# A hand-set opening of a fused decoder block: v's parts and two blocks of q moved ahead of mem's values, norm factors and keys

## The chip, the cores and the metric

The kernel runs on one core of one Trainium2 chip. The metric is the device time of one execution in microseconds (us), as the median of several executions. The profile is of one such execution. PE is the matmul engine, PEld its weight loads, ACT the scalar engine, DVE the vector engine, POOL GpSimd, SP the engine that issues most transfers.

## The reference

One decoder layer over 256 positions of 1024 features, with 256 memory tokens:

```
h    = rmsnorm(x, g_pre_mix)
proj = h @ w_in            # cb, cc, cv, q, k, v (512 columns each), qm (512), three gates (1024 each)
y_a  = (cb * causal_dwconv(cc * cv)) @ w_conv_out
y_b  = attention(q, k, v: 8 heads of 64, causal, position bias) @ w_attn_out
mem_n = rmsnorm(mem, g_mem);  mk, mv = split(mem_n @ w_mem_kv)
y_c  = attention(qm, mk, mv: 4 heads of 128, no mask) @ w_mem_out
x    = x + rmsnorm((sig(ga)*y_a + sig(gb)*y_b + sig(gc)*y_c) @ w_out, g_post_mix)
u    = causal_dwconv(rmsnorm(x, g_pre_ffn) @ w_up);  a, g = split(u)
out  = x + rmsnorm((gelu(a) * g) @ w_down, g_post_ffn)
```

The sequence is one block long, so the block selection of the attention has nothing to select: each query sees its own block.

## The kernel before

**Arithmetic.** Every operand of a matmul is held as two parts, hi (rounded) and lo (the rest). `hilo` makes them: ACT writes hi, then DVE writes lo = value - hi. A product is hi·hi + hi·lo + lo·hi. `wide_blocks` makes a block of 128 output features: 8 matmuls of 512 columns with the weights' hi part (line 237), 8 of 256 columns with their lo part (line 239). After it `add_up` brings the two halves together: ACT copies one half out (`t`, line 244) and DVE adds the other (line 245). After every second block the caller's `evac` runs; `q_evac` is 2 ACT copies (line 502) and 2 DVE operations (line 503).

**Weights.** They come as a list of pieces, in the order of use: 0 to 7 are the memory values' weights, 8 to 11 the memory keys', 12 to 15 v's, 16 to 19 q's (one block each), 20 to 23 k's, 24 to 27 those of the memory queries. `split_until` makes a piece's two parts (line 211 on ACT, line 212 on DVE); five buffers hold the parts of normal pieces, so piece n takes the buffer of piece n - 5. `weights()` is called once for each piece used and asks for the splits of the next three pieces as well; in v's loop it asks for two. Raw pieces are loaded by SP, two in a transfer, and from piece 18 on into three buffers in turn.

**The first stretch.** A region set by hand (`manual_schedule`, from line 421) fixes the order of PE, ACT and DVE *among the instructions written inside it*. Where instructions written behind it fall between them is left to the scheduler of the framework, which draws up each engine's order when the kernel is built; at run time each engine issues in that order. Inside the region stand: the memory values (`pmv`, 2 accumulators), x's norm and its transposes into `hT`, the memory keys (`mk_raw`), and v (`pv`, line 468). Then come, on lines 469 to 478:

- `rm`: two squares of `m_sb` on ACT (line 288) with two small POOL operations each: 1/rms of each memory token
- `mv`: `pmv` scaled by `rm`, as hi and lo (lines 260, 264)
- `spread(diagonals(rm))`: DVE makes two diagonal tiles `dg` (line 296), PE multiplies each with ones (`sp`, line 303; each shows as two matmul records), DVE copies the result to `rms` (line 305)
- `mk`: the two pairs of raw keys times `rms` (line 476), as hi and lo; then `bgh` (line 478)

**Behind the region**, and so placed by the scheduler: two POOL memsets and the load of `bias`, v's parts `vp` in the tile `vk` (`hilo` of `pv`, lines 260 and 262), the four blocks of q and the four of k (lines 513, 514), then the attention's heads with the remaining projections as filler between their steps. The first PE work of the heads is `sc` (lines 537, 538), in the accumulators that `pmv` and `pv` used.

Of the kernel before, what the change touches and what calls it, by code (L numbers as in the profile page):

```python
# [11 lines left out]
F32 = mybir.dt.float32  # L12
F32R = mybir.dt.float32r
BF16 = mybir.dt.bfloat16
AF = mybir.ActivationFunctionType
ALU = mybir.AluOpType
# [3 lines left out]
P = 128  # L20
D = 1024
S = 256
KT = D // P
NT = S // P
H = 8
DH = 64
HM = 4
CW = 512
# [68 lines left out]
def trunk(ctx, tc, x, mem, memT_in, weights_in, par_in, bias_in, g_post_mix, g_post_ffn, out):  # L97
    nc = tc.nc
    const = ctx.enter_context(tc.tile_pool(name="const", bufs=1))
    sb = ctx.enter_context(tc.tile_pool(name="sb", bufs=1))  # L100
# [5 lines left out]
    def tok(t):  # L106
        return slice(t * P, (t + 1) * P)

    def f32(ap):
        return ap.bitcast(F32)  # L110

    def bank(name="mm"):
        return ps.tile([P, 512], F32, tag="mm", name=name, bufs=4)
# [4 lines left out]
    def parts_tile(n, tag, name):  # L118

        return sb.tile([P, n, 2, S], F32R, tag=tag, name=name).rearrange("p k a s -> p a k s")  # L120
# [94 lines left out]
    def weights(hold=False, ahead=AHEAD):  # L215

        nonlocal used, freed
        if not hold:
            freed = used
        split_until(used + 1 + ahead)  # L220
        used += 1
        return parts[used - 1]
# [9 lines left out]
    def mm_wide(p, wh, wl, a):  # L232


        kt = wh.shape[1]
        for k in range(kt):
            nc.tensor.matmul(p, wh[:, k], a[:, :, k], start=(k == 0), stop=False)  # L237
        for k in range(kt):
            nc.tensor.matmul(p[:, :S], wl[:, k], a[:, 0, k], start=False, stop=(k == kt - 1))  # L239

    def add_up(dst, p, tag="t", bufs=2):

        t = wk.tile([P, S], F32, tag=tag, name="t", bufs=bufs)
        nc.scalar.activation(t, p[:, S:], AF.Copy)  # L244
        nc.vector.tensor_tensor(dst, p[:, :S], t, ALU.add)  # L245
# [12 lines left out]
    def hilo(hi, lo, src, scale=1.0):  # L258

        nc.scalar.activation(hi, src, AF.Copy, scale=scale)  # L260
        if isinstance(scale, float) and scale == 1.0:
            nc.vector.tensor_tensor(lo, src, f32(hi), ALU.subtract)
        else:
            nc.vector.scalar_tensor_tensor(lo, src, scale, f32(hi), op0=ALU.mult, op1=ALU.subtract)

    def small(name, n=1):
        return wk.tile([P, n], F32, tag=f"small{n}", name=name, bufs=8)
# [17 lines left out]
    def rstd_row(src, name):  # L285
        ss, se, r = small("ss"), small("se"), small(name)
        junk = wk.tile([P, D], F32, tag="pT", name="junkd", bufs=2)
        nc.scalar.activation(junk, src, AF.Square, scale=D ** -0.5, accum_out=ss)
        nc.gpsimd.tensor_scalar(se, ss, EPS, None, op0=ALU.add)
        nc.gpsimd.tensor_tensor(r, se, mhalf, op=ALU.pow)  # L290
        return r
# [60 lines left out]
    def wide_blocks(nb, a, evac, dst=None):  # L352

        y, wh, wl = None, None, None
        for b in range(nb):
            if wh is None:
                wh, wl = weights()
                at = 0
            p = bank("ft")
            mm_wide(p, wh[:, :, at:at + P], wl[:, :, at:at + P], a)  # L360
            at += P
            if at == wh.shape[2]:
                wh = None
            if b % 2 == 0:
                y = wk.tile([P, 2, S], F32, tag="y", name="y", bufs=YB) if dst is None else dst[:, b:b + 2]
            add_up(y[:, b % 2], p)
            if b % 2:
                evac(b - 1, y)
            yield
# [14 lines left out]
    def run(gen):  # L384
        for _ in gen:
            pass
# [9 lines left out]
    hT = parts_tile(KT, "B", "hT")  # L396
# [12 lines left out]
    with tc.manual_schedule(engines={mybir.EngineType.SP}):  # L409
        for what in "w0 w1 w2 w3 m46 w4 w5 m68 w6 w7 w8 x0 x1 w9 p w10 w11 w12 w13 t0 t1".split():  # L410
            if what[0] == "m":
                a, b = (KT + int(c) * S for c in what[1:])
# [5 lines left out]
            else:  # L418
                t = int(what[1])
                nc.sync.dma_start((x_sb if what[0] == "x" else m_sb)[:, t], (x if what[0] == "x" else mem)[tok(t)])  # L420
    with tc.manual_schedule(engines={mybir.EngineType.PE, mybir.EngineType.Activation, mybir.EngineType.DVE}):
        nc.scalar.activation(small("preload"), mhalf, AF.Exp)
        pw = bank("pw")

        def keep_warm(n):
            one = nc.const_aps.tensor(1.0, (P, 512), BF16)
            for _ in range(n):
                nc.tensor.matmul(pw, one[:, :P], one, start=True, stop=True)

        def mem_part(k):  # L430
            hilo(memT[:, 0, k], memT[:, 1, k], rawT[:, k], gm[:, k:k + 1])

        keep_warm(9)
        nc.vector.tensor_scalar_mul(memT[:, 0, 0], rawT[:, 0], gm[:, 0:1])
        nc.vector.scalar_tensor_tensor(memT[:, 1, 0], rawT[:, 0], gm[:, 0:1], f32(memT[:, 0, 0]), op0=ALU.mult,
                                       op1=ALU.subtract)
        split_until(1)
        mem_part(1)
        split_until(2)
        for k in range(KT):  # L440
            wh, wl = weights(ahead=1)
            if k == 0:
                for n, (a, w) in enumerate(((0, wh), (1, wh), (0, wl))):
                    for t in range(NT):
                        nc.tensor.matmul(pmv[t], memT[:, a, 0, tok(t)], w[:, 0], start=(n == 0), stop=False)
            else:
                values(pmv, memT, k, wh[:, 0], wl[:, 0])
            if k + 2 < KT:
                mem_part(k + 2)
                split_until(k + 3)  # L450
        rx = [rstd_row(x_sb[:, 0], "rx")]
        split_until(9)
        rx.append(rstd_row(x_sb[:, 1], "rx"))
        for t in range(NT):
            nc.vector.tensor_scalar_mul(xn[:, t], x_sb[:, t], rx[t])
            split_until(10 + t)
        gen = blocks(4, memT, mk_evac)
        next(gen)
        next(gen)
        scaled(hT, turned(xn, range(0, 4)), gp)  # L460
        next(gen)
        scaled(hT, turned(xn, range(4, KT)), gp)
        run(gen)
        pv = acc("pv")
        for k in range(0, KT, 2):
            wh, wl = weights(ahead=2)
            for j in range(2):
                values(pv, hT, k + j, wh[:, j], wl[:, j])
        rm = [rstd_row(m_sb[:, t], "rm") for t in range(NT)]
        mv = sb.tile([P, 2, NT, CW], F32R, tag="E", name="mv")  # L470
        for t in range(NT):
            hilo(mv[:, 0, t], mv[:, 1, t], pmv[t], rm[t])
        rms = spread(diagonals(rm), "rms")
        mk = sb.tile([P, 2, HM, S], F32R, tag="mk", name="mk")
        for b, y in zip(range(0, HM, 2), mk_raw):
            nc.vector.tensor_tensor(y, y, twice(rms), ALU.mult)
            hilo(mk[:, 0, b:b + 2], mk[:, 1, b:b + 2], y)
        nc.vector.tensor_scalar_mul(bgh, bg, 0.5)


    vk = sb.tile([P, 4, 1024], F32R, tag="A", name="vk")
    vp = vk[:, :2].rearrange("p a (t c) -> p a t c", c=CW)
    kl = vk[:, 2:].rearrange("p j (n s) -> p j n s", s=S)
    bias = sb.tile([P, H, S], F32, tag="bias", name="bias")
    with tc.manual_schedule(engines={mybir.EngineType.Pool}):
        for j, r in enumerate((slice(0, DH), slice(DH, P))):
            nc.gpsimd.memset(f32(kl[r, 1 - j]), 0.0)
        nc.gpsimd.dma_start(bias, bias_in)
    for t in range(NT):
        hilo(vp[:, 0, t], vp[:, 1, t], pv[t])  # L490

    qk = sb.tile([P, 2, 4, 2, S], F32R, tag="C", name="qk")
    q2, k2 = qk[:, 0], qk[:, 1]
    HEAD = (slice(0, DH), slice(DH, P))

    def q_evac(b, p):
        for j, r in enumerate(HEAD):  # L500
            hi, src = q2[r, b:b + 2, j], p[r]
            nc.scalar.activation(hi, src, AF.Copy, scale=DH ** -0.5)
            nc.vector.scalar_tensor_tensor(q2[HEAD[1 - j], b:b + 2, j], src, DH ** -0.5, f32(hi), op0=ALU.mult,
                                           op1=ALU.subtract)

    def k_evac(b, p):
        for j, r in enumerate(HEAD):
            hi, src = k2[r, b:b + 2, j], p[r]
            nc.scalar.activation(hi, src, AF.Copy)
            nc.vector.tensor_tensor(kl[r, j, b:b + 2], src, f32(hi), ALU.subtract)  # L510
            nc.vector.tensor_copy(k2[HEAD[1 - j], b:b + 2, j], f32(hi))

    run(wide_blocks(4, hT, q_evac))
    run(wide_blocks(4, hT, k_evac))


# [15 lines left out]
    def attend(pair):  # L532
# [30 lines left out]
        mm3(two(po)[:, :, P:], v[1], [pT1[:, b].rearrange("p (j s) -> p j s", s=P) for b in range(2)], False, True)  # L563
        for j, r in enumerate(HEAD):
            hilo(oT[r, 0, pair], oT[r, 1, pair], two(po)[r, j])
# [289 lines left out]
```

## Time and profile before

| | us |
|---|---|
| median of 3 executions (lowest, highest) | 447.78 (447.72, 448.78) |
| the profiled execution | 447.71 |
| its span, first to last instruction | 445.8 |
| PE busy in it | 434.2 |
| PE idle by the page (445.8 - 434.2) | 11.6 |

The span is 1.9 us shorter than the execution's own time. "Busy" of PE is modelled from pipelined matmuls, so the start times of neighbouring matmuls are the better clock.

### The profile page before, as it was taken

What the parts mean: (1) busy time and instruction counts of PE and PEld (TensorE: products, weight loads), DVE (VectorE), ACT (ScalarE), POOL (GpSimd) and SP (SyncE); (2) the same over time, 40 slices, a digit from 0 to 9 for tenths busy, and PEclk for the clock granted to TensorE, in tenths of its full rate; (3) what the DMA queues carried; (4) which work ended last, traced back from release to release, by engine and by line L of the source; (5) the groups of instructions that cost most, each with busy time, mean ns of one, the idle gap of its engine ahead of it and who ended that gap; (6) DMA issues with size and microseconds to landing.
All of it is one profiled execution on the core that took longest, in us unless ns stands there. A gap on an engine that the chain in (4) does not pass through costs nothing.

```text
span 445.8 us, 6664 instructions
## 1 busy us (share of the span) xinstructions
PE 434.2 (97%) x2423; PEld 375.4 (84%) x2423; DVE 358.2 (80%) x634; ACT 292.5 (66%) x526; POOL 13.2 (3%) x35
## 2 busy tenths in 40 slices
PE   8998999999999999999999899999999999999994
PEld 4997888888888988888888698888888888888883
DVE  5787889869986787798686679997879878878875
ACT  6787676757677766666655568866657657657642
POOL 0121000000000000000000300000000000000001
PEclk9999999999999999999999999999999999999998
DMA  8997454543535453455857046556556546546102
GB/s 273 410 419 295 150 191 161 190 160 128 185 122 196 156 187 109 177 190 190 278 193 285 1 159 224 185 188 201 187 182 200 190 176 202 190 175 206 79 1 94
DMA packets 14288, 83.38 MB, mean 187 GB/s; under 512 B 1584, under 2 KB 2096, under 8 KB 5424
## 3 DMA queue, kind: packets, MB, share of 16 engines
q1 hardware_dynamic: 13536, 80.34, 50.5%
q10 hardware_dynamic: 576, 1.58, 1.1%
q0 software_dynamic: 144, 1.05, 0.6%
q8 instruction: 19, 0.31, 0.3%
q14 instruction: 13, 0.11, 0.1%
HBM read 81.91 MB, written 1.05 MB: 186 GB/s over the span
## 4 chain that ended last, share of the span: by engine, by line
PE 95%; ACT 1%; DVE 1%; DMA 1%; issue 0%; POOL 0%; POOLq 0%; DVEq 0%; ACTq 0%
PE ft L237 42%; PE ft L239 21%; PE pf L251 13%; PE po L251 5%; PE pmv L251 2%; PE pv L251 2%; PE po L256 1%; DMA raw<-in_weights_dram 1%; PE ft L229 1%; PE ft L228 1%; PE ft L230 1%; PE at L256 1%; ACT wh L211 1%; PE tp L315 1%; PE ft L377 0%
## 5 line engine op out<-in xcount | busy, mean ns | idle before, releaser
L211 ACT ACTIVATE wh<-raw 128x1024 fp32r<-128x1024 f32 (+1 forms) x139 | 143.3, 1034 | 103.7 <-PE ft L237 71.5
L212 DVE TENSOR_TENSOR wl<-raw,wh 128x1024 fp32r<-128x1024 f32 (+1 forms) x139 | 165.4, 1192 | 53.5 <-ACT wh L211 51.7
L237 PE MATMUL ft<-hT,wh 128*128 128x512 f32 x384 | 97.3, 393 | 0.0
L237 PE MATMUL ft<-h2T,wh 128*128 128x512 f32 x328 | 82.2, 392 | 0.0
L237 PEld LDWEIGHTS ft<-hT,wh 128*128 128x128 f32 x384 | 68.9, 189 | 12.2
L237 PEld LDWEIGHTS ft<-h2T,wh 128*128 128x128 f32 x328 | 59.5, 189 | 11.0
L239 PEld LDWEIGHTS ft<-hT,wl 128*128 128x128 f32 x384 | 52.2, 190 | 3.7
L239 PE MATMUL ft<-hT,wl 128*128 128x256 f32 x384 | 53.6, 282 | 0.0
L244 ACT ACTIVATE t<-ft 128x256 f32<-128x256 f32 x116 | 42.9, 372 | 10.4 <-PE ft L239 10.3
L251 PE MATMUL pf<-wh,f 128*128 128x512 f32 x176 | 49.2, 390 | 0.0
L239 PEld LDWEIGHTS ft<-h2T,wl 128*128 128x128 f32 x328 | 44.9, 190 | 3.3
L239 PE MATMUL ft<-h2T,wl 128*128 128x256 f32 x328 | 45.9, 282 | 0.0
L251 PEld LDWEIGHTS pf<-wh,f 128*128 128x128 f32 x176 | 32.4, 188 | 6.2
L245 DVE TENSOR_TENSOR y<-ft,t 128x256 f32<-128x256 f32 x68 | 28.2, 419 | 2.9 <-ACT t L244 2.6
L251 PE MATMUL pf<-wl,f 128*128 128x512 f32 x88 | 27.5, 390 | 0.0
L748 ACT ACTIVATE u<-v,par 128x256 f32<-128x256 f32 x44 | 24.0, 589 | 3.8 <-DVE v L742 3.8
L597 DVE SCALAR_TENSOR_TENSOR u<-v,par,u 128x255 f32<-128x255 f32 x44 | 19.7, 479 | 0.7 <-ACT u L748 0.7
L598 DVE SCALAR_TENSOR_TENSOR u<-v,par,u 128x254 f32<-128x254 f32 x44 | 19.7, 478 | 0.1
L251 PEld LDWEIGHTS pf<-wl,f 128*128 128x128 f32 x88 | 16.5, 188 | 3.5
L245 DVE TENSOR_TENSOR v<-ft,t 128x256 f32<-128x256 f32 x44 | 18.0, 418 | 0.5 <-ACT t L244 0.5
L251 PE MATMUL po<-wh,mg 128*128 128x512 f32 x64 | 17.9, 389 | 0.0
L251 PEld LDWEIGHTS po<-wh,mg 128*128 128x128 f32 x64 | 11.9, 188 | 2.4
(175 smaller groups left out, 534.8 us busy)
## 6 DMA issues: line engine op xcount, KB each, us to landing
raw<-in_weights_dram SPq DMA_DIRECT2D x66, 1024.0 KB, 4.8
raw<-in_weights_dram SPq DMA_DIRECT2D x8, 256.0 KB, 5.4
rawx<-in_weights_dram SPq DMA_DIRECT2D x4, 512.0 KB, 9.0
rawx<-in_weights_dram SPq DMA_DIRECT2D x2, 1024.0 KB, 12.5
raw<-in_weights_dram SPq DMA_DIRECT2D x2, 512.0 KB, 7.3
x_sb<-in_x_dram SPq DMA_DIRECT2D x2, 512.0 KB, 7.4
m_sb<-in_mem_dram SPq DMA_DIRECT2D x2, 512.0 KB, 9.8
bias<-in_bias_dram POOLq DMA_DIRECT2D x1, 1024.0 KB, 8.9
```

The source lines that it names most:

```text
L211: nc.scalar.activation(hi, v, AF.Copy)
L212: nc.vector.tensor_tensor(lo, v, f32(hi), ALU.subtract)
L228: nc.tensor.matmul(dst, wh[:, k], ah[:, k], start=(k == 0), stop=False)
L237: nc.tensor.matmul(p, wh[:, k], a[:, :, k], start=(k == 0), stop=False)
L239: nc.tensor.matmul(p[:, :S], wl[:, k], a[:, 0, k], start=False, stop=(k == kt - 1))
L244: nc.scalar.activation(t, p[:, S:], AF.Copy)
L245: nc.vector.tensor_tensor(dst, p[:, :S], t, ALU.add)
L251: nc.tensor.matmul(d, a, w[:, c:c + 512], start=(first and w is wh and a is ah), stop=(last and a is al))
L256: nc.tensor.matmul(dst, a[i], b[j], start=(first and n == 0), stop=(last and n == 2))
L597: nc.vector.scalar_tensor_tensor(t[:, 1:], src[:, :S - 1], w1, t[:, 1:], op0=ALU.mult, op1=ALU.add)
L598: nc.vector.scalar_tensor_tensor(t[:, 2:], src[:, :S - 2], w0, t[:, 2:], op0=ALU.mult, op1=ALU.add)
L748: nc.scalar.activation(d, v[:, i], AF.Identity, bias=bb, scale=w2)
```

## The change

The definitions of `vk`, `bias`, `qk`, `q_evac` and `k_evac` move up into the hand-set region. In it, v's parts and the first two blocks of q (with their splits of weights, `add_up` and one `q_evac`) now stand between the squares of `m_sb` and `mv`. The last two blocks of q and all of k stay behind the region. No operation is added or taken away.

```diff
@@ -467,6 +467,40 @@
                 values(pv, hT, k + j, wh[:, j], wl[:, j])
         rm = [rstd_row(m_sb[:, t], "rm") for t in range(NT)]
+        vk = sb.tile([P, 4, 1024], F32R, tag="A", name="vk")
+        vp = vk[:, :2].rearrange("p a (t c) -> p a t c", c=CW)
+        kl = vk[:, 2:].rearrange("p j (n s) -> p j n s", s=S)
+        bias = sb.tile([P, H, S], F32, tag="bias", name="bias")
+        with tc.manual_schedule(engines={mybir.EngineType.Pool}):
+            for j, r in enumerate((slice(0, DH), slice(DH, P))):
+                nc.gpsimd.memset(f32(kl[r, 1 - j]), 0.0)
+            nc.gpsimd.dma_start(bias, bias_in)
...
+        qk = sb.tile([P, 2, 4, 2, S], F32R, tag="C", name="qk")
...
+        for t in range(NT):
+            hilo(vp[:, 0, t], vp[:, 1, t], pv[t])
+        gen = wide_blocks(4, hT, q_evac)
+        next(gen)
+        next(gen)
         mv = sb.tile([P, 2, NT, CW], F32R, tag="E", name="mv")
         for t in range(NT):
             hilo(mv[:, 0, t], mv[:, 1, t], pmv[t], rm[t])
@@ -476,41 +510,7 @@
         nc.vector.tensor_scalar_mul(bgh, bg, 0.5)
-
-
-    vk = sb.tile([P, 4, 1024], F32R, tag="A", name="vk")
...
-    for t in range(NT):
-        hilo(vp[:, 0, t], vp[:, 1, t], pv[t])
...
-    run(wide_blocks(4, hT, q_evac))
+    run(gen)
     run(wide_blocks(4, hT, k_evac))
```

## Rows read from the trace of the kernel before

**Rows 1.** the page: busy time, and the chain that ended last

```profile
PE 434.2 (97%) x2423; PEld 375.4 (84%) x2423; DVE 358.2 (80%) x634; ACT 292.5 (66%) x526; POOL 13.2 (3%) x35
...
PE 95%; ACT 1%; DVE 1%; DMA 1%; issue 0%; POOL 0%; POOLq 0%; DVEq 0%; ACTq 0%
```

**Rows 2.** stretches: length, busy us (instructions) by engine, granted clock, DMA share

```profile
41.50:43.50 2.00, 0.70 (x5) 0.47 (x4) 2.00 (x5) 1.82 (x3) 0.00 (x0) 1.00 0.56 139
43.50:84.00 40.50, 40.50 (x239) 35.69 (x238) 36.20 (x73) 27.11 (x50) 0.00 (x0) 1.00 0.49 175
84.00:90.00 6.00, 5.86 (x36) 4.99 (x35) 4.93 (x14) 4.36 (x10) 0.00 (x0) 1.00 0.53 178
```

**Rows 3.** timeline of PE: start, length, what, count, idle before and its releaser

```profile
41.37 0.39 PE L251 MATMUL pv<-wh,hT 128*128 128x512 f32 x1
43.06 0.46 PE L303 MATMUL sp<-dg,ones 128*128 128x128 f32 x2 [1.30 <-DVE dg L296]
43.27 2.09 PE L237 MATMUL ft<-hT,wh 128*128 128x512 f32 x8
45.20 1.11 PE L239 MATMUL ft<-hT,wl 128*128 128x256 f32 x8
...
46.38 0.38 PE L303 MATMUL sp<-dg,ones 128*128 128x128 f32 x2
...
49.18 2.00 PE L237 MATMUL ft<-hT,wh 128*128 128x512 f32 x8
...
54.76 2.00 PE L237 MATMUL ft<-hT,wh 128*128 128x512 f32 x8
```

**Rows 4.** timeline of ACT around the end of v

```profile
39.08 1.06 ACT L211 ACTIVATE wh<-raw 128x1024 fp32r<-128x1024 f32 x1 [0.57 <-PE pv L251]
40.04 1.25 ACT L260 ACTIVATE mv<-pmv,rm 128x512 fp32r<-128x512 f32 x2
41.18 1.21 ACT L260 ACTIVATE vk<-pv 128x512 fp32r<-128x512 f32 x2
...
46.36 0.37 ACT L244 ACTIVATE t<-ft 128x256 f32<-128x256 f32 x1
...
53.03 1.27 ACT L502 ACTIVATE qk<-y 64x512 fp32r<-64x512 f32 x2
```

**Rows 5.** timeline of DVE before and behind the end of v

```profile
32.47 3.55 DVE L212 TENSOR_TENSOR wl<-rawx,wh 128x1024 fp32r<-128x1024 f32 x3 [0.57 <-ACT wh L211]
37.50 1.22 DVE L212 TENSOR_TENSOR wl<-raw,wh 128x1024 fp32r<-128x1024 f32 x1 [1.48 <-ACT wh L211]
40.17 1.23 DVE L212 TENSOR_TENSOR wl<-raw,wh 128x1024 fp32r<-128x1024 f32 x1 [1.45 <-ACT wh L211]
41.31 1.40 DVE L264 SCALAR_TENSOR_TENSOR mv<-pmv,rm,mv 128x512 fp32r<-128x512 f32 x2
42.63 0.47 DVE L296 TENSOR_SCALAR dg<-ident,rm 128x128 f32<-128x128 f32 x2
43.02 1.28 DVE L262 TENSOR_TENSOR vk<-pv,vk 128x512 fp32r<-128x512 f32 x2
44.22 1.21 DVE L212 TENSOR_TENSOR wl<-raw,wh 128x1024 fp32r<-128x1024 f32 x1
```

**Rows 6.** groups of DVE from 42 to 72: count, busy, mean ns, idle before

```profile
L212 DVE TENSOR_TENSOR wl<-raw,wh 128x1024 fp32r<-128x1024 f32 x10 | 12.2, 1224 | 3.2 <-ACT wh L211 3.1
L245 DVE TENSOR_TENSOR y<-ft,t 128x256 f32<-128x256 f32 x9 | 3.8, 419 | 0.0
...
L296 DVE TENSOR_SCALAR dg<-ident,rm 128x128 f32<-128x128 f32 x2 | 0.5, 278 | 0.0
```

**Rows 7.** waits of PE over the whole span: us in total, times, longest

```profile
PE sp L303 <- DVE dg L296: 1.3, 1, 1.3
...
PE ft L237 <- DVE y L245: 0.2, 1, 0.2
```

**Rows 8.** page, part 6: a load of two pieces, us to landing

```profile
raw<-in_weights_dram SPq DMA_DIRECT2D x66, 1024.0 KB, 4.8
```

More of the change, by code (lines that the diff above doesn't have):

```diff
@@ L469, in trunk, with q_evac, k_evac @@
         rm = [rstd_row(m_sb[:, t], "rm") for t in range(NT)]
+        vk = sb.tile([P, 4, 1024], F32R, tag="A", name="vk")
[7 more added lines that the diff above has]
+        qk = sb.tile([P, 2, 4, 2, S], F32R, tag="C", name="qk")
+        q2, k2 = qk[:, 0], qk[:, 1]
+        HEAD = (slice(0, DH), slice(DH, P))
+        def q_evac(b, p):
+            for j, r in enumerate(HEAD):
+                hi, src = q2[r, b:b + 2, j], p[r]
+                nc.scalar.activation(hi, src, AF.Copy, scale=DH ** -0.5)
+                nc.vector.scalar_tensor_tensor(q2[HEAD[1 - j], b:b + 2, j], src, DH ** -0.5, f32(hi), op0=ALU.mult,
+                                               op1=ALU.subtract)
+        def k_evac(b, p):
+            for j, r in enumerate(HEAD):
+                hi, src = k2[r, b:b + 2, j], p[r]
+                nc.scalar.activation(hi, src, AF.Copy)
+                nc.vector.tensor_tensor(kl[r, j, b:b + 2], src, f32(hi), ALU.subtract)
+                nc.vector.tensor_copy(k2[HEAD[1 - j], b:b + 2, j], f32(hi))
+        for t in range(NT):
[3 more added lines that the diff above has]
+        next(gen)
         mv = sb.tile([P, 2, NT, CW], F32R, tag="E", name="mv")
@@ L478, in trunk @@
         nc.vector.tensor_scalar_mul(bgh, bg, 0.5)
-    vk = sb.tile([P, 4, 1024], F32R, tag="A", name="vk")
[L482 to L488, printed above, removed]
-    for t in range(NT):
-        hilo(vp[:, 0, t], vp[:, 1, t], pv[t])
[L495 to L511, printed above, removed]
-    run(wide_blocks(4, hT, q_evac))
+    run(gen)
     run(wide_blocks(4, hT, k_evac))
```

## The prediction

> **What bounds the kernel now.** I read the page first: PE is busy for 434.2 us of a span of 445.8, and 95% of the chain that ended last lies on PE [rows 1]. So only time in which PE stands still, or matmuls that go away, can move the end; other engines matter where they make PE wait. Next the list of PE's waits: behind the opening there is one of note before the two sub-layers meet, `sp` waiting 1.3 us for DVE's `dg`; among the blocks the only other is a `ft` matmul with 0.2 us [rows 7]. (Nothing before v moves, and the stop between the two sub-layers and the tail are the same code.) Then the table by stretch, to see whether the engine makes up for that wait: from 41.5 to 43.5 PE is busy for 0.70 of 2.00 us, at full granted clock, and from 43.5 to 84 for 40.50 of 40.50 [rows 2]. A saturated engine has nothing to make it up with, so time won at 41.5 should reach the end, as long as nothing opens behind it.
>
> The timelines tell why it waits. v's last matmul starts at 41.37; matmuls of this size follow each other at 0.23 us, so the next could start at 41.60. It starts at 43.06: 1.46 us lost, of which the view lists 1.30 as idle, since the last matmul's end lies at 41.76 [rows 3]. The matmul that waits is `sp`, in its hand-set place. Behind it on PE stands q's first block, and that could have run: its weight parts are among three splits that DVE ended at 36.02 [rows 5], and all of v's matmuls have read `hT` already. What `sp` waits for is a string of steps: ACT splits a piece at 39.08, when v's matmuls give up its buffer; then ACT writes `mv` from 40.04 to 41.29 [rows 4], DVE writes mv's lo parts from 41.31 and `dg` from 42.63, the first of the two ending near 42.9 [rows 5].
>
> **The change, part by part.** Operations stay the same in number and size, so the sum has only order in it.
>
> *Two q blocks ahead of `sp` on PE.* They need nothing that is late, so q's first block starts at 41.60 in place of 43.27 less the two `sp` records. Gain: 1.46 us. Its lower bound by the view's own idle is 1.30; I take 1.46, from start to start.
>
> *`sp` behind them.* The two products of 0.46 and 0.38 us [rows 3] stay and cost what they did. The question is their wait. A block takes 2.79 us (49.18 to 54.76 for two) [rows 3], so q's second block is issued by 41.60 + 5.58 = 47.18. `mv` now stands behind that block's `q_evac` on ACT and DVE. Before, q's first block began at 43.27 and ACT took its result at 46.36, 3.09 later [rows 3, 4]; so here ACT takes the second at 41.60 + 2.79 + 3.09 = 47.48. From there: `t` 0.37, DVE's sum 0.42, `q_evac` on ACT 1.27 for two, `mv` on ACT 1.25 for two, the last lo part of `mv` 0.7, the first `dg` 0.28 [rows 4, 5, 6], together 4.29, and some 0.15 for the hand-overs: `dg` is there at about 51.9. If PE's order has `sp` directly at 47.18, PE stands for 4.7 us; behind q's third block (49.97) for 1.9; behind the fourth (52.76) not at all. The third and fourth blocks are the scheduler's to place, and it does place such work between hand-set instructions: the second `sp` stands at 46.38 behind 17 matmuls of q, though its `dg` was ready 0.2 us after the first one's [rows 3, 5]. Bounds of the wait: 0 and 4.7 us. I take 0, by that row; that the scheduler let the first `sp` stand in front of ready work is the row against it, and gives the first two rivals below.
>
> *A rule that speaks against the change.* The row shows PE standing at 41.76 to 43.06 with q's first block ready behind it [rows 3]. The Trainium skill, page "TensorE: Matmul & The Clock Gate", section "Step-by-step: what each phase is for", says that matmuls stay in program order and only weight loads are drawn ahead. The trace agrees, and by that rule a hand-set `sp` straight behind two q blocks would block the third as `sp` blocked the first; the sum would then be a loss of 4.7 - 1.46 = 3.2 us in place of a gain of 1.46.
>
> *v's parts ahead of `mv`.* ACT can start on the first of v's accumulators near 41.1, as before (41.18) [rows 4]. Their first reader is the second product of the first attention head, behind that head's scores and softmax, so their place costs nothing by itself.
>
> *Splits of pieces 18, 19 and 20, now hand-set behind v's parts.* Before, 18 and 19 were made in slack during v: their lo parts ended at 38.72 and 41.40 [rows 5]. Now ACT comes to 18 when v's parts are written, 41.18 + 1.21 = 42.4, and needs 1.06; DVE has ended v's lo parts by then (41.75 + 1.28) and needs 1.22: ready at 44.7 [rows 4, 5]. q's third block wants it at 47.18, 2.5 us later. On DVE piece 19 ends at 45.9, the first block's sum at 46.3 and piece 20 at 47.5; k's first block wants 20 at 52.76. No wait, but the lead shrinks. DVE still owes at 43 what it had done by then before: two lo parts (2.45), `mv` (1.40) and `dg` (0.47), 4.3 us in all; it starts on v's parts 1.27 us earlier (41.75 against 43.02 [rows 5]), so it runs 3.0 us later by the clock and 4.5 us later against PE. Piece 20 used to be ready at 45.43 for a block at 54.76, a lead of 9.3 us [rows 3, 5]; 4.8 are left. Of 30 us between 42 and 72 DVE idled for 3.2 ahead of its splits alone [rows 6], with which it can win the lead back. Cost 0. What hides it is that lead, thinnest at piece 18; if the order puts one more split's worth of other work ahead of it there, PE waits out 1.06 + 1.22 - 2.5 at worst, that is hardly at all, and with two such pieces of work 2.1 us. Bounds 0 and 2.1.
>
> *Loads.* Pieces 18 and 19 hold a raw buffer some 4.5 us longer, to about 46, so the pair 24 and 25 lands at about 50.8, 4.8 us after its issue [rows 8]; eight blocks behind 41.60 PE comes to block 24 at 64. Cost 0, with a cover of 13 us less one split's 2.3.
>
> *`mk`, `bgh`, the accumulators.* All come some 9 us later. `mk` is first read by the memory heads, behind all four attention pairs; `bgh` is wanted by the first gate and `pmv`'s two accumulators by the first `sc`, which needs all of the first two k blocks. The POOL memsets and the load of `bias` wait for the memory keys' matmuls, which don't move. Cost 0.
>
> Sum: 447.71 - 1.46 = 446.25 for the profiled execution. That execution lies 0.07 below the median of the three, so the median comes to 446.3 us, 0.33% less.
>
> **The rivals.** *The wait comes back in part* (27%): the scheduler puts `sp` behind the third block only, or DVE's lag makes PE wait once or twice. For it: the scheduler's order let `sp` stand 1.46 us before ready work, so it took DVE to be earlier than DVE is, over a string of just four steps; the new string has six. Against: the 40.50 of 40.50 behind it, where all of PE's order was the scheduler's. Price 0.5 to 1.9, so 446.8 to 448.2, with 447.4 as its middle: no change that can be measured, which is also what a change that doesn't do what it says looks like.
>
> *`sp` keeps its hand-set place straight behind the second block* (15%): PE stops for 4.7 us at 47.2 and nothing gives it back: 447.78 + 3.2 = 451.0; with a few matmuls of the third block in front it falls towards 449. The point from which it decides: with `sp` reached at 51.9 - 1.46 = 50.4, shortly into the fourth block, the new wait eats just what the old one gave; each matmul that it stands earlier costs its own length. Against it: nothing holds the third block, whose weights are ready at 44.7.
>
> *More is won* (12%): the scheduler draws up everything behind the region anew, and PE's small losses further on (0.14 us in 84 to 90 [rows 2], the 0.2 us of rows 7) go too: 445.6 to 446.0.
>
> **How the numbers follow.** The plain case has 46%; its own range is 445.9 to 446.8, for small gains and losses of up to 0.4 us in an order drawn up anew. A measurement of this kernel can tell about 0.3% (1.34 us) from no change, so the line lies at 446.44, just above my number: of the plain case two thirds fall below it (0.31) and the rest above; the case of more won adds 0.12; together faster 0.43. The wait that comes back (0.27), the rest of the plain case (0.15) and the mildest of the second rival (0.01) are no change: 0.43. Slower by over 0.3%, over 449.1: 0.14. The range that leaves out 2 in 10 goes from 445.7 to 449.0: it drops the tip of the best case and most of the slow one.
>
> **What would show it.** Right: on PE an `ft` matmul at 41.6 with no idle time before it; `dg` on DVE at about 51.7; `sp` behind at least the third block of q, without idle time; 43.5 to 84 still full; DVE with less idle time before line 212 up to 72. Wrong: an idle time of PE before `sp` at 47 to 52 (first or second rival, by its length), `ft` matmuls waiting for a split of line 212 between 50 and 75, or new gaps among the attention's steps behind 84.

## The result and the profile after

| | before | after |
|---|---|---|
| median, us (lowest, highest; executions) | 448.28 (447.72, 449.02; 4) | 456.51 (455.0, 457.11; 4) |
| profiled execution, us | 447.71 | 456.29 |
| its span, us | 445.8 | 454.3 |

The ratio is 1.0177, with a 95% interval of 1.0159 to 1.0194: 1.8% slower. It is taken over all executions, so it is not the quotient of the two medians (1.0184). The forecast was 446.3, with a range from 445.7 to 449.0.

First PE's list of waits, after (us in total, times, longest). In [rows 7] the same line said 1.3.

```profile
PE sp L303 <- DVE dg L296: 6.3, 1, 6.3
```

PE's timeline, after, from the end of v (start, length, what, count, idle before and its releaser); [rows 3] is the same stretch of before:

```profile
42.38 0.39 PE L251 MATMUL pv<-wh,hT 128*128 128x512 f32 x1
42.61 1.98 PE L237 MATMUL ft<-hT,wh 128*128 128x512 f32 x8
...
47.22 1.11 PE L239 MATMUL ft<-hT,wl 128*128 128x256 f32 x8
54.67 0.77 PE L303 MATMUL sp<-dg,ones 128*128 128x128 f32 x2 [6.34 <-DVE dg L296]
55.09 3.76 PE L237 MATMUL ft<-hT,wh 128*128 128x512 f32 x8
58.65 1.87 PE L239 MATMUL ft<-hT,wl 128*128 128x256 f32 x8
...
60.50 2.07 PE L237 MATMUL ft<-hT,wh 128*128 128x512 f32 x8
```

The old stop is gone: q's first block begins 0.23 us behind v's last matmul. But `sp` stands straight behind q's second block and waits 6.34 us, and no matmul of the third block is in front of it. Behind the stop the third block takes 55.09 to 60.50, 5.4 us in place of 2.79. The table by stretch, after, says why (length, busy us (instructions) of PE, PEld, DVE, ACT, POOL; granted clock; DMA share, GB/s); [rows 2] is that of before:

```profile
41.50:43.50 2.00, 2.00 (x10) 1.67 (x9) 0.74 (x2) 1.29 (x3) 0.00 (x0) 1.00 0.00 0
...
48.20:54.60 6.40, 0.13 (x2) 0.00 (x0) 5.67 (x10) 3.40 (x6) 0.00 (x0) 0.92 0.78 312
54.60:60.50 5.90, 5.83 (x20) 5.08 (x21) 0.12 (x1) 1.06 (x1) 0.00 (x0) 0.51 0.00 0
60.50:66.00 5.50, 5.50 (x34) 4.84 (x33) 4.78 (x7) 2.84 (x5) 0.00 (x0) 1.00 0.53 191
...
84.00:90.00 6.00, 6.00 (x39) 5.26 (x38) 5.96 (x18) 3.93 (x11) 0.00 (x0) 1.00 0.49 173
```

PE's granted clock is 0.51 behind the stop, the lower of its two levels (1.2 GHz), and full again from 60.5. The Trainium skill, page "TensorE: Matmul & The Clock Gate", section "What's actually happening", lists the lower level as that of an engine that has been idle; the 0.51 behind a stop of 6.34 us agrees.

What `sp` waits for, on DVE's timeline, after ([rows 5] is before):

```profile
42.76 1.38 DVE L262 TENSOR_TENSOR vk<-pv,vk 128x512 fp32r<-128x512 f32 x2 [5.73 <-ACT vk L260]
44.39 2.36 DVE L212 TENSOR_TENSOR wl<-raw,wh 128x1024 fp32r<-128x1024 f32 x2 [0.25 <-ACT wh L211]
46.67 0.42 DVE L245 TENSOR_TENSOR y<-ft,t 128x256 f32<-128x256 f32 x1
47.00 3.49 DVE L212 TENSOR_TENSOR wl<-raw,wh 128x1024 fp32r<-128x1024 f32 x3
50.41 0.42 DVE L245 TENSOR_TENSOR y<-ft,t 128x256 f32<-128x256 f32 x1
...
52.92 1.41 DVE L264 SCALAR_TENSOR_TENSOR mv<-pmv,rm,mv 128x512 fp32r<-128x512 f32 x2
54.25 0.47 DVE L296 TENSOR_SCALAR dg<-ident,rm 128x128 f32<-128x128 f32 x2
```

and on ACT's, after:

```profile
48.71 0.37 ACT L244 ACTIVATE t<-ft 128x256 f32<-128x256 f32 x1
50.86 1.28 ACT L488 ACTIVATE qk<-y 64x512 fp32r<-64x512 f32 x2 [1.78 <-DVE y L245]
52.17 1.27 ACT L260 ACTIVATE mv<-pmv,rm 128x512 fp32r<-128x512 f32 x2
```

The string is the one that the prediction laid out, with one item more: ACT's `t` of the second block ends at 49.08, but DVE comes to the sum only at 50.41, since its order has three lo parts (pieces 20, 21 and 22) in a row ahead of it. No data in these rows held the third block back: the lo parts of pieces 18 and 19 had ended at 46.75, and the sum of the first block, the last reader of its bank, at 47.09.

**The account.** Compare where PE begins q's fourth block: 51.97 before, 60.50 after, 8.53 later; the profiled times differ by 8.58, so all of it lies here. The opening, which the change does not touch, took 1.01 longer in this execution (v's last matmul at 42.38 against 41.37). The old stop gives back 1.46. From the end of the second block's slot (47.22 + 0.95 = 48.17) to `sp` (54.67) are 6.50. The block at the lower clock costs 5.41 - 2.79 = 2.62. 1.01 - 1.46 + 6.50 + 2.62 = 8.67; the rest, -0.14, lies in the `sp` products and in the first blocks.

### The profile page after: what moved, and what is told of

Read it like the earlier page. It is cut to its first block, busy times and chain, and to the rows that moved or that the text cites. A ratio compares the mean times of both kernels' runs of the same rounds, so it can differ in the third digit from the quotient of the medians.

```text
span 454.3 us, 6664 instructions
## 1 busy us (share of the span) xinstructions
PE 437.7 (96%) x2423; PEld 379.0 (83%) x2423; DVE 358.2 (79%) x634; ACT 292.9 (64%) x526; POOL 13.2 (3%) x35
## 4 chain that ended last, share of the span: by engine, by line
PE 94%; DVE 2%; ACT 1%; DMA 1%; issue 0%; POOL 0%; POOLq 0%; DVEq 0%; ACTq 0%
PE ft L237 41%; PE ft L239 21%; PE pf L251 13%; PE po L251 5%; PE pv L251 2%; PE pmv L251 2%; PE po L256 1%; DMA raw<-in_weights_dram 1%; PE ft L229 1%; PE ft L228 1%; PE ft L230 1%; DVE wl L212 1%; PE pmv L445 1%; PE at L256 1%; ACT wh L211 1%; PE tp L315 1%
## 5 line engine op out<-in xcount | busy, mean ns | idle before, releaser
L237 PE MATMUL ft<-hT,wh 128*128 128x512 f32 x384 | 98.9, 398 | 0.0
L237 PEld LDWEIGHTS ft<-hT,wh 128*128 128x128 f32 x384 | 70.1, 192 | 12.6
L237 PEld LDWEIGHTS ft<-h2T,wh 128*128 128x128 f32 x328 | 59.5, 189 | 11.0
```

## The experiments

Theory A: `sp` takes its bank from the same tag of PSUM buffers ("mm", four of them) as the blocks' `ft`, and the framework's order lets no later user of that tag pass it; so what is late at `sp` stops PE, and the clock falls behind the stop. Theory B: q's blocks pass freely, and it is the lag of ACT and DVE in splitting weights that costs. Ratios are to the kernel before, timed beside each run. A `...` in a diff stands for lines left out; in runs 4 to 7 they also give `diagonals(rm)` a line of its own straight ahead of `spread`, which leaves the order as it is.

**1. The changed kernel, `sp` in a bank of the accumulators' tag.**

```diff
-        p = bank("sp")
+        p = ps.tile([P, 512], F32, tag="acc", name="sp", bufs=4)
```

> The changed kernel with one line altered: sp takes its PSUM bank from the accumulators' tag, not from the tag that the ft blocks share. In the new order of PE six blocks of q and k stand ahead of sp in place of two. Theory A (the loss is PE held by sp, which keeps the third block from going ahead because both draw on one tag's banks in program order; the clock falls in that stop): no wait at sp, no half-speed block, near 446.5 us, 0.3 to 0.4% below the kernel before. Theory B (the reordered DVE and ACT work, five splits ahead of the second block's sum, is what costs): PE waits for splits or sums between 47 and 60 even so, and the time stays at 450 or more.

Measured: 447.11 us, 0.9971 [0.996, 0.9982]. PE's timeline of this kernel:

```profile
42.33 0.39 PE L251 MATMUL pv<-wh,hT 128*128 128x512 f32 x1
42.55 1.98 PE L237 MATMUL ft<-hT,wh 128*128 128x512 f32 x8
...
59.04 0.61 PE L303 MATMUL sp<-dg,ones 128*128 128x128 f32 x4
```

Nearly six blocks now stand ahead of `sp`, which waits for nothing. The tag is all that differs, and `sp` is still written inside the region, so its place was the tag's doing and not the region's: 9.4 us between the two kernels' medians. A new wait shows in PE's list for this kernel, when the attention begins:

```profile
PE po L256 <- ACT pT L260: 0.7, 1, 0.7
```

**2. The same line in the kernel before.**

> The kernel before with the same one line altered; no work is moved in the source. PE's order then has q's first block and most of the second ahead of sp. Theory A: the wait of 1.3 us at sp goes, and the time falls by 1.4 to 1.5 us, to about 0.997 of before, without any of the change. Theory B says nothing against that. A third theory (the wait at sp in the kernel before was hidden by later slack, so its removal is worth nothing): ratio 1.000.

Measured: 446.54 us, 0.9963 [0.9951, 0.9975]. PE's timeline of this kernel:

```profile
41.62 0.39 PE L251 MATMUL pv<-wh,hT 128*128 128x512 f32 x1
41.85 1.98 PE L237 MATMUL ft<-hT,wh 128*128 128x512 f32 x8
...
46.57 0.61 PE L303 MATMUL sp<-dg,ones 128*128 128x128 f32 x4
```

The old stop is gone with nothing moved by hand: the scheduler puts `sp` into the second block's matmuls. The 1.46 us of the prediction are there to be had, and no stop takes their place. This is the lowest median of all kernels run; its interval overlaps those of runs 1, 3, 7 and 9.

**3. `mv` and `dg` ahead of v's parts and of q; `sp` still behind the two blocks.**

```diff
+        mv = sb.tile([P, 2, NT, CW], F32R, tag="E", name="mv")
+        for t in range(NT):
+            hilo(mv[:, 0, t], mv[:, 1, t], pmv[t], rm[t])
+        dg = diagonals(rm)
         for t in range(NT):
             hilo(vp[:, 0, t], vp[:, 1, t], pv[t])
...
-        mv = sb.tile([P, 2, NT, CW], F32R, tag="E", name="mv")
-        for t in range(NT):
-            hilo(mv[:, 0, t], mv[:, 1, t], pmv[t], rm[t])
-        rms = spread(diagonals(rm), "rms")
+        rms = spread(dg, "rms")
```

> The changed kernel with mv and the diagonals put back ahead of v's parts and of the two q blocks; only spread and mk stay behind the q blocks, so dg is made while PE works on them. sp keeps its place behind two blocks and its tag. Theory A: dg is ready near 43 and sp is reached at 47, so no wait: ratio about 0.997. Theory B (the splits and v's parts moved behind the squares cost by themselves): dg early, yet PE waits for the third block's split, ratio 1.000 or more.

Measured: 447.5 us, 0.9983 [0.9972, 0.9994]. `sp` goes at 47.95 without a wait, in the same place. So the place costs nothing when `dg` is early. But PE's list of this kernel shows a wait further on:

```profile
PE po L256 <- ACT pT L260: 1.1, 1, 1.1
```

This is a cost of the kind that theory B expects, though not where it expects it; that the late splits cause it is not shown by this run.

**4. The changed kernel, the stop filled** with 28 bf16 products of ones whose result nobody reads.

```diff
         next(gen)
         next(gen)
+        pw2 = bank("pw2")
+        one = nc.const_aps.tensor(1.0, (P, 512), BF16)
+        for _ in range(28):
+            nc.tensor.matmul(pw2, one[:, :P], one, start=True, stop=True)
...
```

> The changed kernel with 28 extra matmuls of ones (bf16, 512 columns, their result not used) between the second q block and sp: at 0.22 us each they fill 6.0 of the 6.5 us that PE stands. The stop itself stays, so this prices the clock alone. Theory A with the clock: the block behind sp runs at full pitch, 2.8 us in place of 5.3, and the time falls by 2.4 to 2.9 us against the changed kernel, to about 453.8. If the slow block has another cause (weights or loads that are late): no difference, 456.5.

Measured: 453.39 us, 1.0115 [1.0094, 1.0137]. PE's timeline of this kernel:

```profile
47.20 6.30 PE L507 MATMUL pw<-const-bfloat16-1.0 128*128 128x512 bf16 x28
53.71 0.46 PE L303 MATMUL sp<-dg,ones 128*128 128x128 f32 x2 [0.20 <-DVE dg L296]
53.92 2.09 PE L237 MATMUL ft<-hT,wh 128*128 128x512 f32 x8
```

`sp` comes as late as ever behind the second block (53.71 - 47.20 = 6.51), yet the next block runs at full pace, at a granted clock of 1.00 from 53.7 to 59.5. The stop's length is thus not all of its cost: keeping PE busy won 3.1 us between the medians, and `sp` with the block behind it accounts for 2.6 of it. The medians rest on four executions each, and the opening moves single ones by 1 us or more (last section).

**5. Half of the change: v's parts ahead of `mv`, q left to the scheduler.** In the kernel before, the definitions move up as in the change, and:

```diff
+        for t in range(NT):
+            hilo(vp[:, 0, t], vp[:, 1, t], pv[t])
         mv = sb.tile([P, 2, NT, CW], F32R, tag="E", name="mv")
...
```

> The kernel before with only v's parts moved ahead of mv in the hand-set region; all of q stays behind the region and sp keeps its tag. Theory A (PE can pass sp with nothing that draws on the ft tag's banks after it, and what stands ahead of dg on ACT and DVE is PE's wait): mv now follows v's parts on ACT (end near 42.4 in place of 40.0 for the start), so dg comes near 44.6 and sp waits about 3 us in place of 1.46: about 1.5 us slower, ratio 1.003 to 1.004. A theory that v's parts are harmless: ratio 1.000.

Measured: 452.22 us, 1.0076 [1.0061, 1.0092]. PE's timeline and the stretch behind the stop, in this kernel:

```profile
46.20 0.46 PE L303 MATMUL sp<-dg,ones 128*128 128x128 f32 x2 [3.01 <-DVE dg L296]
46.41 2.87 PE L237 MATMUL ft<-hT,wh 128*128 128x512 f32 x8
```

```profile
46.20:50.80 4.60, 4.60 (x19) 4.04 (x20) 1.19 (x2) 1.06 (x1) 0.00 (x0) 0.64 0.14 53
```

The wait was as expected, the time not: the granted clock behind it is 0.64, and the block to 50.78 takes 4.37 us in place of 2.79, 1.6 more. This stop lowered the clock too.

**6. All four blocks of q ahead of `mv`.**

```diff
         next(gen)
         next(gen)
+        next(gen)
+        next(gen)
...
```

> The changed kernel with all four q blocks, not two, by hand ahead of mv. A theory of cover (two blocks were too little work to hide dg, four are enough) expects the wait at sp to shrink by 5.6 us, that is to go, and a time near 446.5. Theory A expects no gain: mv now hangs behind the fourth block's sum and parts, no k block may pass sp, so PE waits there for about 5 to 6.5 us as before and the clock falls again: 455 to 457.

Measured: 456.21 us, 1.0174 [1.0156, 1.0191]. PE's timeline of this kernel, then the stretch behind the stop:

```profile
59.93 0.77 PE L303 MATMUL sp<-dg,ones 128*128 128x128 f32 x2 [6.87 <-DVE dg L296]
```

```profile
60.00:65.60 5.60, 5.60 (x18) 4.83 (x19) 0.00 (x0) 1.06 (x1) 0.00 (x0) 0.50 0.00 0
```

Twice the work ahead of `sp` does not shorten the wait: `mv` stands behind the last of it, and the string to `dg` begins only there. More cover, written ahead of the whole string, is no cover. PE's list of this kernel also has `po` waiting 1.1 us for `pT`, as in run 3.

**7. The region ended behind q's two blocks; `mv`, `dg`, `sp` and `mk` left to the scheduler.** The lines stay where they are, one level out.

```diff
-        mv = sb.tile([P, 2, NT, CW], F32R, tag="E", name="mv")
...
+    mv = sb.tile([P, 2, NT, CW], F32R, tag="E", name="mv")
```

> The changed kernel with the hand-set region ended behind the two q blocks: mv, dg, sp, mk are left to the scheduler. In its order dg stands early on DVE, ahead of v's parts, and on PE sp still stands straight behind the second block, though nothing but the tag holds it there. Theory A: dg is ready long before 47, no wait at sp, ratio 0.996 to 0.998. If the place of sp behind just two blocks costs in itself: ratio above 1.000.

Measured: 447.28 us, 0.9972 [0.9961, 0.9983]. On PE `sp` stands at 47.91, again straight behind the second block, without a wait. DVE's timeline of this kernel:

```profile
37.65 0.29 DVE L296 TENSOR_SCALAR dg<-ident,rm 128x128 f32<-128x128 f32 x1 [0.87 <-POOL rm L290]
...
39.09 0.28 DVE L296 TENSOR_SCALAR dg<-ident,rm 128x128 f32<-128x128 f32 x1
```

The scheduler, free to choose, makes `dg` over 15 us earlier than the changed kernel does: `dg` needs `rm` alone. No third block passes `sp` here either, but since `sp` was ready there was nothing to gain by it: that the tag and not the region holds the blocks back rests on runs 1 and 2.

**8. The changed kernel, the split of piece 21 asked for by hand behind `dg`.** `split_until(22)` makes the pieces up to 21; up to 20 they were asked for already.

```diff
+        dg = diagonals(rm)
+        split_until(22)
-        rms = spread(diagonals(rm), "rms")
+        rms = spread(dg, "rms")
```

> The changed kernel with the split of piece 21 written by hand behind the diagonals; piece 22's then falls behind it too, so DVE makes one lo part in place of three between the sums of the two q blocks. The second block's sum waited 1.3 us for these; with them gone dg should come 1.6 us earlier, the wait at sp fall from 6.3 to about 4.8, and the time by about 1.6 us against the changed kernel, to 454.9. If the three splits were hidden behind the wait for the second block's matmuls: no difference, 456.5.

Measured: 454.38 us, 1.0116 [1.01, 1.0132]. PE's timeline of this kernel, then DVE's:

```profile
53.40 0.77 PE L303 MATMUL sp<-dg,ones 128*128 128x128 f32 x2 [4.72 <-DVE dg L296]
```

```profile
47.34 1.22 DVE L212 TENSOR_TENSOR wl<-raw,wh 128x1024 fp32r<-128x1024 f32 x1
```

With one lo part between the two sums in place of three the wait is 4.72 us (4.89 from the end of the second block's slot to the start of `sp`): 1.6 shorter, and near the 4.7 that the prediction had as its upper bound.

**9. The kernel before, `dg` written ahead of `mv`.**

```diff
+        dg = diagonals(rm)
         mv = sb.tile([P, 2, NT, CW], F32R, tag="E", name="mv")
...
-        rms = spread(diagonals(rm), "rms")
+        rms = spread(dg, "rms")
```

> The kernel before, with the two `dg` tiles written ahead of `mv`; nothing else moves. `dg` is computed from `rm` alone, and in the kernel with `mv` left to the scheduler DVE made the two at 37.65 and 39.09 us. Theory (what sp waited for was not data but DVE's order, in which `dg` stood behind `mv`, a string that hangs on the pieces of weights): no wait at sp, q's first block some 0.2 us behind v's last matmul's slot, the whole gain of about 1.4 us without moving q: 448.78 median of before less 1.4 = 447.3, ratio 0.997. Rival (dg is not early enough in that place, since rm's second half itself is late): sp still waits up to 1.3 us, ratio 1.000.

Measured: 447.42 us, 0.9971 [0.9958, 0.9983]. PE's timeline of this kernel, then DVE's:

```profile
42.85 0.39 PE L251 MATMUL pv<-wh,hT 128*128 128x512 f32 x1
43.08 0.38 PE L303 MATMUL sp<-dg,ones 128*128 128x128 f32 x2
43.21 2.09 PE L237 MATMUL ft<-hT,wh 128*128 128x512 f32 x8
```

```profile
40.98 0.29 DVE L296 TENSOR_SCALAR dg<-ident,rm 128x128 f32<-128x128 f32 x1 [0.78 <-POOL rm L290]
...
42.79 1.40 DVE L264 SCALAR_TENSOR_TENSOR mv<-pmv,rm,mv 128x512 fp32r<-128x512 f32 x2
```

The stop of the kernel before was DVE's order, not data: with `dg` ahead of `mv` it is gone, and `sp` keeps its place and its bank.

**10. The changed kernel, `dg` written ahead of v's parts; `mv` stays where the change put it.**

```diff
+        dg = diagonals(rm)
         for t in range(NT):
             hilo(vp[:, 0, t], vp[:, 1, t], pv[t])
...
-        rms = spread(diagonals(rm), "rms")
+        rms = spread(dg, "rms")
```

> The changed kernel, with the two `dg` tiles written ahead of v's parts; `mv` stays behind q's two blocks. Theory (the stop at sp is the string of steps that DVE's order sets ahead of dg; with dg out of that string nothing is left of it, whatever bank sp takes): no wait at sp straight behind q's second block, full clock behind it, 447.0 to 447.6, ratio 0.996 to 0.9975. Rival (mv's own lateness matters, or attention's first steps wait for the lagging DVE by 0.5 to 1 us as in the kernel with mv first): 447.5 to 448.3, ratio 0.9975 to 0.999, with a wait at po near 85 us.

Measured: 451.71 us, 1.0063 [1.0044, 1.0083]: slower than both expected. PE's timeline of this kernel, then its table by stretch:

```profile
48.64 0.61 PE L303 MATMUL sp<-dg,ones 128*128 128x128 f32 x4
...
84.67 0.28 PE L539 MATMUL sc<-vk,qk 128*128 128x256 f32 x1
86.31 0.59 PE L552 MATMUL pp<-ident,e 128*128 128x128 f32 x2 [1.35 <-DVE e L531]
...
88.20 0.63 PE L256 MATMUL po<-pT,vk 128*128 128x512 f32 x1 [1.20 <-ACT pT L260]
88.63 3.49 PE L237 MATMUL ft<-hT,wh 128*128 128x512 f32 x8
```

```profile
54.00:84.00 30.00, 30.00 (x181) 26.65 (x180) 29.17 (x57) 22.40 (x39) 0.00 (x0) 1.00 0.53 180
84.00:90.00 6.00, 3.45 (x17) 2.49 (x16) 4.75 (x20) 3.09 (x13) 0.00 (x0) 0.87 0.38 154
```

The stop at `sp` is gone as theory A has it, and a cost of theory B's kind appears in its place. DVE idles 3.53 us ahead of v's parts in this kernel (39.70 to 43.23), with everything that is written by hand behind them waiting too; it is then busy for 29.17 of 30 us up to 84 (27.33 in run 9) and still late: PE waits 1.35 and 1.20 us in the attention's first steps, and the block behind them (88.63 to 92.90) takes 4.27 in place of 2.79. Against the profiled 447.71 of before: -1.46, +2.55, +1.48, and 1.48 from an opening that was longer in this execution (its first block begins at 43.08, where 41.60 was the place in before) make 4.05, of 4.22 measured (451.93).

DVE's lag alone does not explain it. The same stretch of run 1, which waits 0.7 us only, and PE's timeline there:

```profile
54.00:84.00 30.00, 30.00 (x181) 26.69 (x180) 29.43 (x62) 22.03 (x39) 0.00 (x0) 1.00 0.52 182
```

```profile
83.79 0.28 PE L538 MATMUL sc<-vk,qk 128*128 128x256 f32 x1
83.91 0.52 PE L239 MATMUL ft<-hT,wl 128*128 128x256 f32 x3
```

DVE is at least as full there (29.43 of 30). What differs is PE's order: between the last of these `sc` and `po` it has three matmuls of a block in run 1, nine in runs 3 and 7, 26 in run 9, which does not wait there at all, and none in run 10. The scheduler left PE nothing to do while `pp` and `po` wait; why it drew that order is open.

## Why the prediction was wrong

**Right: the gain.** PE was the bound, the old stop was 1.46 us, and a saturated PE hands a gain on to the end: runs 2 and 9, which remove nothing but the stop, won 0.37% and 0.29%, where 1.46 us are 0.33%.

**The step that failed: "Bounds of the wait: 0 and 4.7 us. I take 0, by that row."** The row was the second `sp`, placed behind 17 matmuls. It shows that the second product can be put off among blocks; it does not show that a block written behind `spread` can pass the first. The row that did bear on it stood beside it and was called "the row against it": the first `sp` in front of ready work, in the kernel before. The prediction looked for what holds the third block in its weights and found nothing; it did not look at where `sp` gets its buffer. The third block's weights were indeed ready (46.75 at the latest), and runs 1 and 2 show that it is the tag that held it. That the framework hands out a tag's buffers in the order of the program is my reading of these orders; how it does so was not looked into. The rule that the prediction weighed against itself, that matmuls stay in program order on the engine, was borne out, and the outcome is its second rival, which had 15%.

**A term that was mis-sized: the wait.** 4.7 was worked out for the string alone; 6.5 came, because the scheduler placed three splits ahead of the second block's sum, where the prediction had one (piece 20). Run 8 takes the other two out and gives 4.89 on the same count, so the string's working was right to 0.2 us and the missing piece was the queue in front of the sum.

**A term that was left out: the clock.** The prediction has no term for it: the rival was priced as 447.78 + 3.2 = 451.0. The block behind the stop cost a further 2.62 us at a granted clock of 0.51, and run 4, which changes only what PE does in the stop, gets it back. With the wait at 6.5 and the clock's 2.6 the rival's own sum would have been 447.78 - 1.46 + 6.5 + 2.6 = 455.4; the median came 1.1 above that, about what the opening varies by, though that it was the opening is shown for the profiled execution only.

**A second step that was wrong and does not show in the changed kernel: "Cost 0" for the splits made later.** PE is full from 84 to 90 there, 6.00 of 6.00. Run 10, without the stop, pays 2.55 us in waits and 1.48 for the clock behind them; runs 1, 3 and 7 show a wait of 0.7, 1.1 and 0.3 in the same steps. The bound of 2.1 was drawn for piece 18; the waits came in the attention, 40 us on. That the changed kernel escapes because the stop gave DVE the time to catch up (busy for 5.67 of 6.40 us with PE standing) is likely but not shown: run 6 has a stop too and waits 1.1 us. How much of run 10's loss is DVE's lag, and how much the order that leaves PE without a block in those steps, was not separated.

**Not contradicted:** the loads, `mk`, `bgh` and the POOL work. PE's list of waits for the changed kernel has no new line; only that of `sp` grew.

## What to carry to other kernels

Before counting on a scheduler to fill a wait, look up which buffers the waiting instruction and the work behind it share: in these kernels, work written later on the same tag did not pass it. When a chain is moved behind other work, time the chain from its new start, with everything that its engines have queued in between, and price a stop of the matmul engine with the clock behind it. And ask first what the late operand needs: here `dg` needed only `rm`, and one line moved up (run 9) or one buffer tag (run 2) won what the larger reordering was after.

## What the runs showed of the hardware that was not expected

**Most stops cost more than their length.** Behind stops of 6.34, 6.87, 4.72 and 3.01 us the granted clock fell (to 0.51, 0.50, 0.62 and 0.64 over the stretch to the end of the next block, or near it, in the changed kernel and runs 6, 8 and 5). Behind the 1.30 us of the kernel before it stayed at 1.00 [rows 2]. Run 10's two short stops, 1.35 and 1.20 us with little work between, were followed by 0.50 from 88.5 to 91.

**The opening varies between executions by 1 to 1.5 us, whatever the kernel.** PE's timeline of the changed kernel, first matmuls of `pmv`:

```profile
6.01 2.05 PE L445 MATMUL pmv<-wh,memT 128*128 128x512 f32 x4 [1.25 <-ACT wh L211]
```

In the profiled execution of before the same four took 1.17 us, as in runs 2, 3, 4, 6 and 7; in those of runs 1, 5, 8, 9 and 10 again 2.04 or 2.05. v's last matmul starts between 41.37 (before) and 42.85 (runs 9 and 10). So a difference of 1 us between two profiled executions is not a difference of the kernels unless it lies behind the opening; the account above takes it out for that reason. The Trainium skill, page "TensorE: Matmul & The Clock Gate", section "What's actually happening", says that the number of slow matmuls at a kernel's start differs from run to run; these rows agree in pace (0.46 us from one matmul to the next here, 0.26 in before). The granted clock is listed as 1.00 for this stretch in both, so it does not show the slow pace.
